# A hybrid block on one core: RG-LRU in its own buffers behind the RWKV's blocks, both pairs of heads in one PSUM bank, six banks for the late output-projection tiles

## The chip, the cores and the metric

The kernel runs on one core of a Trainium2 chip. The metric is the device time of one execution in microseconds (us). Of the kernel before, three runs are shown beside one profiled execution, whose trace gives every instruction of every engine: TensorE (PE, with its weight loads PEld), VectorE (DVE), ScalarE (ACT), GpSimd (POOL), and SyncE (SP), on whose queue nearly all DMAs are issued.

## What is computed

One layer over 2048 tokens, with 16 learned meta tokens put ahead of them, in float32 and of width 1024:

```python
p = rms_norm(h, norm_mix_pre) @ w_in                 # 1024 -> 3080 columns
oa = rg_lru_group(xa, ya, ...)                       # RG-LRU, 256 wide
ob = forgetting_attention_group(q, k, v, f, ...)     # 8 heads of 64, causal, with decay
oc = rwkv7_group(pc, ...)                            # 4 heads of 64, delta rule
h = h + rms_norm(concat(oa, ob, oc) @ w_out, norm_mix_post)
f = causal_dwconv(rms_norm(h, norm_ffn_pre) @ ffn_up, ffn_conv)      # 1024 -> 2 x 2816, 3 taps
h = h + rms_norm((gelu(gate) * val) @ ffn_down, norm_ffn_post)
```

The RG-LRU is a 4-tap convolution `u`, two gates (block-diagonal products with `u`), and a scan `h = a h + sqrt(1 - a^2) (i u)`, times `gelu(ya)`. The RWKV-7 group updates a 64 x 64 state per head and token with a decay, a removal along `kk` and an addition.

## The kernel before, in words

Every large product is made of three single-pass products of split operands (hi x hi, hi x lo, lo x hi; `mm3`, L148 to L152). The stages follow each other in one program, and the builder puts the instructions of each engine in an order of its own: by their place in the program and by when a model of the machine has their operands ready. On the chip every engine takes its list strictly in that order.

**Input projection** (to about 850 us). The tokens are done in three parts. In each part, `w_in_norm` (L165) normalises and transposes the rows, and `w_in_part` (L258) goes through the column blocks: RWKV's eight, RG-LRU's four, then k, v and q. Each unit loads 512 KB of weights, splits them, and multiplies. Results go to scratch in DRAM.

**Recurrences beside it.** `Beside` (L1856) runs a generator, `recurrences` (L1886), whose every `yield` ends one step; after each unit of the projection `advance` takes PACE = 1.5 steps on average. A part has 25 units; its own recurrences are added at unit 14, so that 12 units of each part, and the first 13 of the next, have its steps put beside them. For each part there are two steps of gates for the attention and then three blocks of 256 tokens. For each block:

- `lru_block` (L1333): two steps. The convolution `u`, the two gate products L1359 and L1363, tanh, exp, a square root (L1378), the scan (L1382), and the product with gelu (L1386 to L1391). The gate products and scans are made for each half of the channels (p = 0, 1); everything else runs on both halves at once, 512 elements wide. It borrows the RWKV's buffers `k`, `r`, `sq`, `e` and `raw`.
- `Rwkv.block` (L955): four steps up to SOLVED. `mixed` shifts tokens; L981 and L987 are the decay's and the rate's products, L995 and L1014 those of the norm of the keys, L1034 that of the bonus. Each of the pairs p = 0, 1 of heads takes the bank from `pe()` in turn: there is one, with tag `ae` (L935), so that a product waits until the reader of the one before is through. Then `chunks` (L1039): scores (L1058), transposes (L1087), and a 16-step substitution (L1099 to L1102).
- the ending of the block before: seven steps, from L1111 to the mixed output at L1282, with the state's steps at L1209.

With the two RG-LRU steps a block makes 13 steps. What remains when the projection ends is run by `beside.finish()`, in program order ahead of the attention.

While parts 2 and 3 run, `up_sums` (L1544) makes sums and differences of the up projection's weights for eleven column blocks on POOL: one step loads two tiles of 512 KB, makes four sums, and writes 1 MB; one step is taken in every fourth unit.

**Attention** (about 860 to 1590 us). `Attn.run` goes through the heads twice, first for the queries of blocks 0 and 1, then for 2 and 3 (512 queries each). The products of scores (L635, L636) fall into two banks with tag `sc`, the maxima's into `mx`, the values' into `pv`. The exponentials (L640) go into a ring `p` of NP = 9 buffers of 128 x 512, and are summed by POOL and DVE (L679). Between the two halves `meta` (L543) does the 16 meta rows in buffers of their own.

**Output projection** (`w_out_tile`, L1421), 17 tiles: 2 rows, then 16 of 128. Tiles 0 to 8 need only the first half of the attention and fill its second half; tiles 7 and 8 are held back for its last steps. A tile loads the mixed rows (`load_parts`, L139: ACT's copy L144 and DVE's difference L145 into `mh` and `ml`, two buffers each), makes two halves of 512 columns, and `add_normed` (L1444) squares both (L1450, into `mh` as waste), adds the sums (L1451), takes 1/sqrt by an integer guess and three Newton steps on DVE (`rstd_from`, L80 to L90: nine operations on 128 x 1), scales (L1456) and adds the residual (L1457). `rstd_of` (L93) does the same for the next norm (its square, L96, again into `mh`). `Banks` (L1399) hands out the banks: two, and from tile 8 on three. From tile 8 on, `ffn_norm` (L1484) also prepares the up projection's operands, one tile of rows at a time, and `ffn_sums` (L1517) subtracts the quarters on POOL.

**Up and down projection** (to the end). `ffn_up` (L1643) goes through 3 x 22 units of seven products with three banks each, in turn from two pools; the first unit takes the pool that lies where the output projection's banks were. `Down` (L1756) then makes 8 pairs of row tiles in two passes; `add_normed` closes each tile of the second.

## Time and profile before

| | us |
|---|---|
| runs of the kernel before, median of 3 | 3098.33 |
| lowest and highest | 3095.21 and 3101.57 |
| the profiled execution | 3089.22 |
| its span, first to last instruction | 3087.5 |
| mean granted PE clock | 0.962 |

In the page of the profile, busy time is given per engine with its share of the span and the number of instructions; the rows of digits cut the span into 40 slices of 77 us. The granted clock tells at what share of its full speed PE was let run. In the rows of waits stand the waiting engine, tile and line, what ended the wait, the total in us, how often, and the longest. In the timeline stand the start, the length, the engine, the line, the operation, the tiles (out<-in), and in brackets the engine's idle time just before, with what ended it. Tile names are the program's: `eps` is the bank of `pe()`, `rw...` are the RWKV's buffers, `pswo` the output projection's banks, `psu` the up projection's.

### The profile page before, as it was taken

The numbers are of one execution on the slowest core, as the hardware profiler recorded it, in microseconds if no ns is written. First come the engines' busy times: TensorE is split into PE (matmuls) and PEld (weight loads), VectorE is DVE, ScalarE is ACT, GpSimd is POOL, SyncE is SP. The second block draws the span as 40 slices with busy tenths as digits, with TensorE's granted clock in tenths as the row PEclk, the third lists the DMA queues.
The fourth block names the chain that finished last, engine by engine and source line by source line (L and its number), as shares of the span: only waits on it lengthen the run. The fifth ranks groups of instructions, "written<-read, shape, count | busy, mean of one in ns | idle before, by whom it ended". The sixth has DMA issues, their size and how long they took to land. (4 is left out here: it accounts for less than half of the span.)

```text
span 3087.5 us, 52530 instructions
## 1 busy us (share of the span) xinstructions
PE 2920.0 (95%) x18488; PEld 2490.5 (81%) x18488; DVE 2230.6 (72%) x4574; ACT 1458.1 (47%) x2716; POOL 1320.6 (43%) x1447
## 2 busy tenths in 40 slices
PE   6998999999978899999998899999999999999998
PEld 6997898988856554665576899999999999787776
DVE  5258666777678778778748788787778787547777
ACT  4245333444534444445533556656566665324332
POOL 1001211232124465556733457445645534557665
PEclk9998999999958888999999999999999999999999
DMA  4345544475353335544236456566777765425444
GB/s 142 115 134 166 154 122 133 145 207 170 84 125 76 81 84 136 140 111 115 64 106 201 154 183 181 173 195 209 212 213 215 214 193 180 159 99 169 148 157 143
DMA packets 482520, 463.92 MB, mean 150 GB/s; under 512 B 83808, under 2 KB 391722, under 8 KB 479296
## 3 DMA queue, kind: packets, MB, share of 16 engines
q1 hardware_dynamic: 481872, 460.18, 50.9%
q8 instruction: 145, 2.38, 0.3%
q14 instruction: 119, 0.97, 0.1%
q0 software_dynamic: 384, 0.39, 0.0%
HBM read 334.58 MB, written 125.87 MB: 149 GB/s over the span
## 5 line engine op out<-in xcount | busy, mean ns | idle before, releaser
L150 PE MATMUL psu<-xo,uw 128*128 128x344 f32 x1848 | 590.1, 324 | 14.9 <-DVE wx L1457 4.8
L151 PE MATMUL psu<-xo,uw 128*128 128x344 f32 x1848 | 594.1, 322 | 1.0 <-DVE xo L1529 1.0
L152 PE MATMUL psu<-xo,uw 128*128 128x344 f32 x1848 | 583.4, 321 | 0.0
L152 PE MATMUL psp<-xh,wl 128*128 128x384 f32 (+2 forms) x1152 | 377.3, 328 | 0.0
L150 PE MATMUL psp<-xh,wh 128*128 128x384 f32 (+2 forms) x1152 | 377.3, 328 | 0.0
L151 PE MATMUL psp<-xl,wh 128*128 128x384 f32 (+2 forms) x1152 | 376.9, 327 | 0.0
L150 PEld LDWEIGHTS psu<-xo,uw 128*128 128x128 f32 x1848 | 348.0, 189 | 18.1 <-DVE wx L1457 5.2
L1529 DVE TENSOR_TENSOR uw<-uq,uw 128x512 fp32r<-128x512 f32 x341 | 313.6, 926 | 62.4 <-ACT uw L1528 59.2
L151 PEld LDWEIGHTS psu<-xo,uw 128*128 128x128 f32 x1848 | 349.3, 189 | 1.3 <-DVE xo L1529 1.3
L152 PEld LDWEIGHTS psu<-xo,uw 128*128 128x128 f32 x1848 | 347.8, 189 | 0.0
L1528 ACT ACTIVATE uw<-uq 128x512 fp32r<-128x512 f32 x462 | 287.4, 627 | 107.3 <-PE psu L152 50.6
L640 ACT ACTIVATE p<-sc,bias 128x512 f32<-128x512 f32 (+4 forms) x352 | 197.9, 591 | 206.8 <-PE sc L636 160.8
L1660 DVE SCALAR_TENSOR_TENSOR uy<-psu,ffn_cols,uy 128x342 f32<-128x342 f32 (+1 forms) x396 | 223.6, 567 | 73.1 <-ACT uy L1658 71.9
L679 POOL TENSOR_TENSOR acc<-acc,p 128x512 f32<-128x512 f32 (+3 forms) x208 | 230.3, 1113 | 101.9 <-DVE acc L679 50.4
L1666 POOL TENSOR_TENSOR uy<-uy,uy 128x342 f32<-128x342 f32 (+1 forms) x132 | 141.9, 1075 | 270.5 <-DVE uy L1660 78.9
L1529 POOL TENSOR_TENSOR uw<-uq,uw 128x512 fp32r<-128x512 f32 x121 | 175.6, 1451 | 140.6 <-ACT uw L1528 115.9
L151 PEld LDWEIGHTS psp<-xl,wh 128*128 128x128 f32 x1152 | 217.9, 189 | 7.3 <-issue 5.4
L152 PEld LDWEIGHTS psp<-xh,wl 128*128 128x128 f32 x1152 | 218.0, 189 | 6.7 <-issue 4.9
L150 PEld LDWEIGHTS psp<-xh,wh 128*128 128x128 f32 x1152 | 217.9, 189 | 6.2 <-issue 4.0
L512 DVE TENSOR_REDUCE mc<-mx 128x1 f32<-128x400 f32 (+5 forms) x320 | 171.8, 554 | 58.9 <-PE mx L509 53.2
L1528 ACT ACTIVATE fo<-u 128x896 fp32r<-128x896 f32 x88 | 81.1, 922 | 231.1 <-POOL u L1776 123.5
L1529 DVE TENSOR_TENSOR fo<-u,fo 128x896 fp32r<-128x896 f32 x88 | 103.0, 1172 | 116.1 <-ACT fo L1528 116.1
(453 smaller groups left out, 6628.1 us busy)
## 6 DMA issues: line engine op xcount, KB each, us to landing
uq<-scr_us SPq DMA_DIRECT2D x220, 256.0 KB
uq<-in_ffn_up_dram SPq DMA_DIRECT2D x209, 256.0 KB
raw<-in_w_in_dram SPq DMA_DIRECT2D x72, 512.0 KB
u<-scr_ff SPq DMA_DIRECT2D x88, 256.0 KB
scr_ff<-uy SPq DMA_DIRECT2D x110, 171.0 KB
q<-scr_qh SPq DMA_DIRECT2D x96, 128.0 KB
us<-in_ffn_up_dram SPq DMA_DIRECT2D x22, 512.0 KB
scr_us<-us SPq DMA_DIRECT2D x11, 1024.0 KB
```

The lines of the kernel that those rows point to most:

```text
L150: nc.tensor.matmul(out, ah, bh, start=first, stop=False, skip_group_check=more)
L151: nc.tensor.matmul(out, ah, bl, start=False, stop=False, skip_group_check=more)
L152: nc.tensor.matmul(out, al, bh, start=False, stop=last, skip_group_check=more)
L512: self.reduced = nc.vector.tensor_reduce(mc[:rows, i, ci : ci + 1], ps[:rows, :full], axis=AX.X, op=ALU.max)
L640: last = nc.scalar.activation(p[:rows, :w], ps[:rows, :w], AF.Exp, bias=bias[:rows, j : j + 1])
L679: eng.tensor_tensor(a, ps_[0][0][:rows, c0:n] if start and i == 1 else a, p[:rows, : n - c0], op=ALU.add)
L1528: core.nc.scalar.activation(hi, src, AF.Copy)
L1529: (eng or core.nc.vector).tensor_tensor(lo, src, hi, op=ALU.subtract)
L1660: stt(y[:, :n], src[:, i : n + i], cw[:, 44 * i + cc : 44 * i + cc + 1], y[:, :n], op0=ALU.mult, op1=ALU.add)
L1666: core.pooled = nc.gpsimd.tensor_tensor(v[:, :n], g[:, :n], v[:, :n], op=ALU.mult)
```

## The change

1. `lru_block` now does one half of the channels after the other in four steps, in buffers of its own (`lu`, `lr`, `lg`, `la`, 256 wide, and `lraw`), with both gate products of a half in one bank; and in `recurrences` it stands behind the block and the ending, not ahead of them.
2. In `Rwkv.block` both products of a pair go to the two halves of one bank before either is read; the bonus is one product of 512 columns. With the RG-LRU's that makes 7 turns of the `ae` bank a block in place of 13.
3. PACE is 2.0 in place of 1.5; a block now makes 15 steps.
4. `up_sums` works on half a column block at a time, in half the buffer: 22 steps of four loads, four sums of 256 elements and one write, a step in every second unit.
5. `meta` takes its five larger tiles from the exponentials' ring `p`.
6. From tile 8 on, `Banks` goes round six banks: three of the up projection's first pool, then the two and the one of before. The up projection's first unit takes that first pool (`turn = 1`).
7. From tile 8 on and in the down projection (`core.root`), 1/sqrt is made by DVE (mean), ACT (square root) and DVE (reciprocal).

```diff
+def rstd_root(core, v, sums, width):
+    nc = core.nc
+    ms, y = v[:, 0:1], v[:, 2:3]
+    nc.vector.tensor_scalar(ms, sums[1], 1.0 / width, EPS, op0=ALU.mult, op1=ALU.add)
+    nc.scalar.activation(y, sums[0], AF.Sqrt, scale=1.0 / width, bias=ms)
+    nc.vector.reciprocal(y, y)
+    return y
...
     ss = v[:, 4:5]
+    if core.root:
+        half = width // 2
+        sums = ss, v[:, 5:6]
+        for i, acc in enumerate(sums):
+            cs = slice(half * i, half * i + half)
+            core.nc.scalar.activation(junk[:, cs], src[:, cs], AF.Square, accum_out=acc)
+        return rstd_root(core, v, sums, width)
...
-        new = lambda s: self.t([P, NH, META], s, F32R, 1)
-        q1, q2, q3, k1, k2 = (new("m" + s) for s in ("q1", "q2", "q3", "k1", "k2"))
-        v = self.t([META, NH, 64], "mv", bufs=1)
+        new = lambda shape, dt: self.t(shape, "p", dt, self.NP)
+        q, k = new([P, 3, NH, META], F32R), new([P, 2, NH, META], F32R)
+        (q1, q2, q3), (k1, k2) = (q[:, i] for i in range(3)), (k[:, i] for i in range(2))
+        v = new([META, NH, 64], F32)
...
+        both = lambda ps: [ps[:, p * n : p * n + n] for p in range(2)]
+        for rows, s, out in ((slice(0, 64), "w0_h", sig), (slice(64, 128), "a0_h", av)):
+            ps = both(self.pe())
+            for p in range(2):
+                nc.tensor.matmul(ps[p], k["up"][rows, P * p : P * p + P], flat(wa[:])[rows], start=True, stop=True)
+            for p in range(2):
+                nc.scalar.activation(flat(half(out, p)), ps[p], AF.Tanh, scale=0.5, bias=pcol(s, p))
...
-            ps = self.pe()
-            nc.tensor.matmul(ps[:, :n], k["bones"][:], flat(half(kp, p)), start=True, stop=True)
-            tt(half(bon, p), ps[:, :n].rearrange("p (c t) -> p c t", t=CH), half(rav, p)[:, :, 2], op=ALU.mult)
+        ps = self.pe()[:, : 2 * n]
+        nc.tensor.matmul(ps, k["bones"][:], flat(kp[:]), start=True, stop=True)
+        tt(bon[:], ps.rearrange("p (c t) -> p c t", t=CH), rav[:, :, 2], op=ALU.mult)
...
     def tl(s):
-        return R.t([P, 2, 256], s)[:, :, :n]
+        return R.t([P, 256], s)[:, :n]
...
+    def raw(row, a):
+        t = R.t([P, 260], "lraw", bufs=2)[:, : c0 + n - a]
+        nc.sync.dma_start(t, scr["p"][row : row + P, a : c0 + n])
+        return t
...
     for p in range(2):
         pc = slice(p, p + 1)
+        x = raw(P * p, c0 - 3)
+        u, r, g, al = (tl("l" + s) for s in ("u", "r", "g", "a"))
...
+        pa, px = ps[:, :n], ps[:, 256 : 256 + n]
+        nc.tensor.matmul(pa, k["ga_w"][:, p], u, start=True, stop=True)
+        nc.tensor.matmul(px, k["gx_w"][:, p], u, start=True, stop=True)
...
     def next(self):
-        self.turn = (self.turn + 1) % 3 if self.wide else 0
-        third = self.turn == 2
-        return self.pools[third].tile([P, 512], F32, tag="wo", name=self.core.n("pswo"), bufs=1 if third else 2)
+        if not self.wide:
+            pool, tag, n = self.pools[-2]
+        else:
+            self.turn += 1
+            ring = [p for p in self.pools for _ in range(p[2])]
+            pool, tag, n = ring[self.turn % len(ring)]
+        return pool.tile([P, 512], F32, tag=tag, name=self.core.n("pswo"), bufs=n)
...
+    n = HK // 2
+    for j, z in ((j, n * i) for j in js for i in range(2)):
+        t = pool.tile([P, 4, n, P], F32, tag="us", name=core.n("us"))
+        for i in range(4):
+            r0, c0 = P * (HK * (i % 2) + z), FF * (i // 2) + P * j
+            nc.sync.dma_start(t[:, i], w_up[r0 : r0 + n * P, c0 : c0 + P].rearrange("(k p) c -> p k c", p=P))
...
-    turn = 0
+    turn = 1
...
-PACE = 1.5
+PACE = 2.0
...
     for b in ((0, 1, 2), (3, 4, 5), (6, 7, 8))[part]:
-        yield from lru_block(core, R, scr, lk, b)
         gen = R.block(b)
         while next(gen) != R.SOLVED:
             yield
         yield from R.ending
         R.ending = gen
+        yield from lru_block(core, R, scr, lk, b)
...
-                    if part and i % 4 == 0:
+                    if part and i % 2 == 0:
...
-            banks = Banks(core, ps_wo)
+            banks = Banks(core, [(ps_f[0], "up", 3), (ps_wo[0], "wo", 2), (ps_wo[1], "wo", 1)])
...
-                banks.wide = i >= LATE - 1
+                banks.wide = core.root = i >= LATE - 1
```

More of the change, by code (lines that the diff above doesn't have):

```diff
@@ L45, in __init__ @@
         self.flip = 0
+        self.root = False
     def n(self, s):
@@ L1011, in block @@
         tt(kp[:], kt[:], kp[:], op=ALU.mult)
+        ps = both(self.pe())
         for p in range(2):
[L1013 to L1015 removed]
+            nc.tensor.matmul(ps[p], k["spr"][:, p], kinv, start=True, stop=True)
+        for p in range(2):
+            stt(flat(half(kt, p)), flat(half(kt, p)), pcol("k_k", p), ps[p], op0=ALU.mult, op1=ALU.mult)
         kk = kt[:]
```

110 lines of the change are left out of this document (40 added, 70 removed).

## The prediction

> **What bounds the kernel now.** I read the page first. TensorE (PE) is busy 95% of the span, and the digits show where it isn't: slices 12 to 16, a little in slices 4 and 22, and both ends.
>
> ```profile
> PE 2920.0 (95%) x18488; PEld 2490.5 (81%) x18488; DVE 2230.6 (72%) x4574; ACT 1458.1 (47%) x2716; POOL 1320.6 (43%) x1447
> PE   6998999999978899999998899999999999999998
> PEclk9998999999958888999999999999999999999999
> ```
>
> Busy time alone hides the clock, so I cut the span at the stages' borders and read the table of windows: length, then busy us and instructions of PE, weight loads, DVE, ACT and POOL, then PE's granted clock.
>
> ```profile
> 40.00:275.00 235.00, 234.88 (x1334) 226.66 (x1333) 105.20 (x216) 87.93 (x150) 7.59 (x17) 1.00 0.42 124
> 275.00:310.00 35.00, 22.77 (x105) 19.34 (x104) 30.12 (x66) 19.50 (x35) 7.28 (x6) 0.76 0.69 196
> 310.00:620.00 310.00, 304.66 (x2674) 276.40 (x2674) 200.25 (x433) 126.72 (x224) 60.43 (x75) 0.99 0.48 140
> 620.00:850.00 230.00, 227.31 (x2371) 205.89 (x2365) 164.89 (x360) 104.26 (x191) 49.97 (x60) 0.99 0.54 152
> 850.00:1190.00 340.00, 294.51 (x2365) 196.53 (x2363) 267.79 (x815) 141.36 (x300) 148.79 (x236) 0.78 0.40 96
> 1190.00:1590.00 400.00, 380.51 (x1648) 228.20 (x1649) 298.13 (x700) 199.75 (x353) 247.04 (x265) 0.99 0.42 105
> 1590.00:1725.00 135.00, 114.78 (x516) 94.10 (x514) 108.10 (x244) 51.95 (x94) 34.40 (x27) 0.92 0.53 173
> 1725.00:2610.00 885.00, 877.21 (x5550) 874.71 (x5549) 699.42 (x1093) 546.08 (x1077) 469.07 (x376) 1.00 0.65 196
> 2610.00:3087.00 477.00, 446.97 (x1879) 355.02 (x1877) 324.24 (x497) 163.02 (x262) 285.21 (x359) 0.97 0.45 149
> ```
>
> I call length minus busy times clock the loss: time in which PE did no work at full clock. Beside the input projection (310 to 850) it is 540 - 0.99 x 532 = 13 us, 0.025 a us. In 850 to 1190, where the RWKV's last blocks run beside the attention's first half, it is 340 - 0.78 x 294.5 = 110 us, 0.32 a us, with DVE at 79%. Beside attention and output projection (1190 to 1590) it is 23 us, 0.06 a us. The late tiles (1590 to 1725) lose 135 - 0.92 x 114.8 = 29 us, and the seam of the first two parts (275 to 310) 35 - 0.76 x 22.8 = 18 us. Since the change leaves PE's work almost as it is, only these losses can move. PE's waits, longest first, name some of them.
>
> ```profile
> PE eps L981 <- ACT rwe L982: 12.5, 2, 11.9
> PE pswo L150 <- DVE wx L1457: 11.1, 4, 4.4
> PE psu L150 <- DVE wx L1457: 4.8, 1, 4.8
> ```
>
> **The change, part by part.** *The seam.* The timeline at 287 us shows the longest wait whole.
>
> ```profile
> 285.90 0.68 DVE L1391 SCALAR_TENSOR_TENSOR rwk<-rwk,rwe 128x512 f32<-128x512 f32 x1
> 286.61 0.47 ACT L982 ACTIVATE rwe<-eps,rwkv_om 128x256 f32<-128x256 f32 x1 [2.34 <-DVE rwk L1391]
> 287.14 1.22 PE L981 MATMUL eps<-rwwa,wa_up 64*128 64x256 f32 x2 [11.87 <-ACT rwe L982]
> ```
>
> L1391 is the RG-LRU's last operation, and it reads buffer e. L982 writes the block's first part of e, so it waits for L1391; the second L981 waits for the one bank that L982 reads; all of PE stands behind it. With e no longer shared and one bank for both halves this wait goes, up to 16 of the 18 us. But the next part's norms stand behind it and are late next. I take half: -8 (0 to -16).
>
> *The tail.* These rows give the RWKV's pace: first product of the gates of blocks 6, 7 and 8 (L981), the RG-LRU ahead of block 6 (L1359), two halves of a pair at L981 and at L1034, and the last operation of the recurrence.
>
> ```profile
> 748.24 0.59 PE L1034 MATMUL eps<-rwsq,bones 128*128 128x256 f32 x2
> 767.92 0.59 PE L1034 MATMUL eps<-rwsq,bones 128*128 128x256 f32 x2
> 795.92 0.70 PE L1359 MATMUL eps<-rwk,lru_ga_w 128*128 128x256 f32 x2
> 812.62 0.70 PE L981 MATMUL eps<-rwwa,wa_up 64*128 64x256 f32 x2
> 822.62 0.70 PE L981 MATMUL eps<-rwwa,wa_up 64*128 64x256 f32 x2
> 898.38 1.22 PE L981 MATMUL eps<-rwwa,wa_up 64*128 64x256 f32 x2
> 986.72 0.69 PE L981 MATMUL eps<-rwwa,wa_up 64*128 64x64 f32 x2
> 1180.35 0.20 DVE L1278 TENSOR_TENSOR rwxu<-rwxu,rps 128x64 f32<-128x64 f32 x1
> ```
>
> A block takes 86 and 88 us. The RG-LRU ahead of it is 17 of them (796 to 813), since both use buffers k, r, sq and e; the halves of a pair stand 10 us (L981) and 20 us (L1034) apart, for the bank has to be read in between. A block's 13 turns of that bank become 7. By the written order, 18 steps are put beside the projection's last 12 units, about 4 of them owed to the part before, and they reach block 6 and six of the seven steps of block 5's ending. Afterwards there are 24 with none owed, which reach block 7's solve and three steps of block 6's ending: some 10 of RWKV's 11 steps further, about 80 us of chain. Moved from beside attention to beside the projection, each us brings 0.32 less what its work loses elsewhere (0.68 x 0.05), 0.286: -23. The bounds are 0, if DVE's load and not RWKV's place sets the tail, and -48 for twice the distance.
>
> *The RG-LRU itself.* Ten wide DVE operations and five wide ACT ones a block become twice as many half ones, and each half has its own square root, so each of nine blocks has two table loads more there and back.
>
> ```profile
> L1391 DVE SCALAR_TENSOR_TENSOR rwk<-rwk,rwe x9: 216/680/930, 196.7 to 994.2; 128x512 f32<-128x512 f32 x7, 128x416 f32<-128x416 f32 x1, 128x128 f32<-128x128 f32 x1
> L1361 DVE TENSOR_SCALAR rwe<-eps,lru_cols x18: 268/476/484, 175.0 to 982.5; 128x256 f32<-128x256 f32 x14, 128x208 f32<-128x208 f32 x2, 128x64 f32<-128x64 f32 x2
> L1378 ACT ACT_TABLE_LOAD x9 | 11.5, 1283 | 18.5 <-DVE rwr L1377 18.4
> ```
>
> On DVE 20 x 0.476 - 10 x 0.68 = 2.7 us a block, on ACT two loads, 2.6 us. Beside the projection both lie in idle time of DVE (365 busy of 540) and ACT; in the tail one full block and a small one stay: +3 (0 to +10). The Trainium skill, in "ScalarE: Activation LUTs" under "Table sets: the hidden batching unit", speaks against this: functions are to be grouped by table set, and a switch is put at 2.66 us with its drain. The trace agrees on the load, 1283 ns, and no row here shows a drain; four more switches in the tail at the page's figure would be 11 us, an estimate, and the sum 8 us smaller.
>
> *The late tiles.* With three banks a tile's second half waits for the last tile's first half (11.1 us), and the up projection's first unit for the last tile (4.8 us). Six banks, and that unit on the three freed first, take both away. DVE's chain shortens too: from L1451 to the last L89 it took 1.9 us undisturbed and 6.7 us while POOL worked on the quarters' sums.
>
> ```profile
> 1658.79 0.16 DVE L1451 TENSOR_TENSOR rs<-rs 128x1 f32<-128x1 f32 x1 [0.33 <-ACT mh L1450]
> 1665.34 0.83 DVE L89 SCALAR_TENSOR_TENSOR rs<-rs 128x1 f32<-128x1 f32 x1
> 1700.71 0.16 DVE L1451 TENSOR_TENSOR rs<-rs 128x1 f32<-128x1 f32 x1 [3.28 <-ACT mh L1450]
> 1702.49 0.16 DVE L89 SCALAR_TENSOR_TENSOR rs<-rs 128x1 f32<-128x1 f32 x1
> L150 PE MATMUL pswo<-woh,mh 128*128 128x512 f32 x122 | 50.4, 413 | 11.1 <-DVE wx L1457 11.1
> ```
>
> Ten operations become two with a square root between. What adds a wait: ACT's root now stands behind DVE, and ACT's copies of mh behind the root. Late next is mh: two buffers, the older read last by L96. I take 13 of the 15.9 us and half of the 9 us of half clock: -17 (-8 to -27). Tile 8 now needs banks that the attention's scores hold, so it fills no gap there; 48 products of 0.41 us bound that at +20 (they overlap, so it is less), 0 if attention ends sooner for it, as I assume: it then has PE to itself.
>
> *The meta rows.* Their operands now take five of the nine buffers of the exponentials.
>
> ```profile
> L562 PE MATMUL mx<-mk,mq x8: 170/170/253, 1144.3 to 1144.5; 128*16 128x16 f32 x8
> L587 PE MATMUL mx<-mp,mv x16: 204/204/225, 1159.1 to 1160.8; 16*64 16x16 f32 x16
> ```
>
> They hold them for these 17 us and the loads before, while attention makes do with four: between 0 and all 17. I take +6.
>
> *Costed at nothing.* The up sums in halves:
>
> ```profile
> L1559 POOL TENSOR_TENSOR us<-us 128x512 f32<-128x512 f32 x33 | 49.1, 1487 | 2.2
> SPq L1560 <- POOL us L1559: 18.1, 6, 5.7
> L1552 SPq DMA_DIRECT2D us<-in_ffn_up_dram x22: 378/582/2078, 287.2 to 752.4; - x22
> ```
>
> POOL is idle 430 of 540 us, so 44 more, shorter operations hide there. SP gets 77 issues more here and 27 for the RG-LRU, 104 x 0.58 = 60 us in 700; behind a write that waits for POOL (up to 5.7 us) stand the projection's weights, which are loaded ahead. Without that cover a few us. The root in the last stage is worth -1 in the final chain (+2 to -2).
>
> **Sum**, against the profiled execution (3089.2 us, span 3087.5): -8 - 23 + 3 - 17 + 6 - 1 = -40. That execution lies 9.1 us below the median of the runs, so 3098.3 - 40 = 3058.
>
> **Rivals.** *The tail doesn't shrink* (0.20): attention's first half is held by its own DVE reductions, not by the RWKV beside it. For it speaks DVE's 79%; against it that the RWKV's operations are part of this load. Seam, late tiles and costs remain, with the seam halved again: -4 + 3 - 17 + 6 - 1 = -13, 3085 (3078 to 3102).
>
> *PE stops behind the recurrence* (0.19, slower): steps come at 2.0 a unit in place of 1.5, and PE takes its stream in order; a recurrence product placed ahead of its operands stops the projection, as at 287 us: 11.87 us idle and 0.24 x 22.8 = 5.5 us of clock, 17 in all. Against it: that stop came from the shared e, and 310 to 850 lost only 13 us in all. From the third such stop on it eats the 40 us; with four it gives 3058 + 68 = 3126.
>
> *The six banks bring nothing* (0.07): tiles stay bound to the two buffers of mh and the wait moves from the bank to L145. Then -17 becomes about 0: 3075. And 0.03 is for no change from all that cancels.
>
> **How the numbers follow.** My forecast has 0.51 (3028 to 3083). A measurement of this kernel can tell about 0.2%, 6 us, from no change. Faster: 0.51 + 0.16 of the first rival + 0.07 = 0.74; within 0.2%: 0.04 + 0.03 = 0.07; slower 0.19. The range, 3025 to 3108, leaves out the far end of the tail's gain (0.07) and the worse half of the stops (0.12).
>
> **What would show it.** The wait of L981 for L982 gone, and the clock in 275 to 310 up; block 8's L981 before about 910 instead of 987, and the recurrence's end before 1110; the loss in the stretch from the projection's end to 1190 nearer 85 than 110; no PE wait for wx in the late tiles, tile 16's products ending about 15 us sooner counted from attention's last exponential. I am wrong if the recurrence's end moves and the tail's loss doesn't, or if idle time grows in 310 to 850.

## The result, and the profile after

The changed kernel took 3108.79 us (median of 8 runs, 3105.01 to 3116.63), the kernel before on the same chip 3095.22 us (8 runs, 3091.01 to 3101.57): a ratio of 1.0044 (95% interval 1.0029 to 1.0059). It is slower by 14 us where 40 us less was forecast, and lies 0.8 us above the range. The profiled execution took 3106.46 us, with a span of 3104.7 and a mean granted clock of 0.957.

The page's rows that answer to those of before: TensorE's busy time, then its digits and those of the clock.

```profile
PE 2924.9 (94%) x18470; PEld 2500.8 (81%) x18470; DVE 2188.1 (70%) x4401; ACT 1497.1 (48%) x2833; POOL 1324.0 (43%) x1491
...
PE   6998999999989978999889899999999999999998
...
PEclk9999999989978788999999999999999999999999
```

TensorE is as busy as before, within 5 us; slice 9 (621 to 698 us), beside the projection, had a 9 in the clock and now has an 8. The windows, cut at the changed kernel's own borders (the projection ends at 867, attention's last scores come at 1604, the up projection ends at 2633):

```profile
275.00:310.00 35.00, 26.23 (x312) 22.67 (x311) 28.78 (x73) 19.75 (x37) 13.28 (x19) 0.80 0.73 202
310.00:620.00 310.00, 304.76 (x2534) 276.13 (x2532) 193.61 (x449) 129.19 (x232) 56.67 (x86) 0.99 0.45 133
620.00:867.00 247.00, 237.72 (x2346) 217.98 (x2343) 170.77 (x395) 120.60 (x225) 52.88 (x79) 0.96 0.55 154
867.00:1207.00 340.00, 289.29 (x2338) 194.90 (x2337) 274.18 (x834) 153.80 (x321) 144.19 (x234) 0.79 0.43 104
1207.00:1604.00 397.00, 367.82 (x1544) 217.03 (x1544) 276.46 (x654) 189.27 (x337) 240.44 (x263) 0.96 0.38 91
```

The loss (length minus busy time at full clock, as in the prediction) is 35 - 0.80 x 26.23 = 14 us at the seam (18 before), 8 in 310 to 620 (8), but 247 - 0.96 x 237.72 = 19 from 620 to the projection's end (5), 340 - 0.79 x 289.29 = 111 in the next 340 us (110), and 397 - 0.96 x 367.82 = 44 in the attention's second half (23). So the loss of those 340 us stood still, and two stretches that the forecast had left alone lost 14 and 21 us more. Cut where the recurrence itself ends, the tail reads otherwise: the kernel before up to 1180 and from there to the last scores, then the changed kernel up to 1152 and in the next 55 us.

```profile
850.00:1180.00 330.00, 286.16 (x2329) 192.42 (x2327) 259.75 (x799) 136.34 (x292) 141.93 (x230) 0.78 0.39 93
1180.00:1587.00 407.00, 385.86 (x1668) 230.94 (x1668) 303.97 (x712) 203.79 (x359) 253.71 (x270) 0.99 0.43 108
```
```profile
867.00:1152.00 285.00, 249.88 (x2155) 173.56 (x2153) 236.24 (x742) 133.18 (x285) 129.37 (x211) 0.78 0.39 93
1152.00:1207.00 55.00, 39.40 (x183) 21.34 (x184) 37.95 (x93) 20.62 (x36) 14.82 (x23) 0.79 0.62 163
```

Beside the recurrence the loss is 330 - 0.78 x 286.16 = 107 us before and 285 - 0.78 x 249.88 = 90 us after, 0.32 a us in both. Behind it the kernel before loses 407 - 0.99 x 385.86 = 25 us, but the changed kernel 55 - 0.79 x 39.40 = 24 us in the first 55 us alone, and the 44 in the rest. So the price per us held as long as the recurrence ran; what did not hold is that the attention runs almost without loss where the recurrence is gone.

Stage by stage, each from the last product of one kind to the last of the next in the profiled execution (us):

| | projection ends | recurrence ends | attention | late tiles | up | down | tail | span |
|---|---|---|---|---|---|---|---|---|
| before | 850.0 | 1180.6 | 737.1 | 112.5 | 911.1 | 463.3 | 13.5 | 3087.5 |
| after | 867.4 | 1152.4 | 736.3 | 123.5 | 905.9 | 460.6 | 11.0 | 3104.7 |
| e1 (tile 8 on old banks) | 874.7 | 1159.1 | 736.7 | 110.2 | 909.9 | 457.6 | 11.0 | 3100.1 |
| e14 (six banks, root only) | 852.7 | 1182.5 | 725.1 | 110.2 | 906.1 | 458.6 | 11.1 | 3063.8 |
| e15 (e1, no sums) | 841.9 | 1148.2 | 747.4 | 111.1 | 928.6 | 463.1 | 11.2 | 3103.3 |
| e18 (e1, sums whole) | 863.7 | 1139.9 | 729.1 | 110.3 | 908.8 | 459.6 | 11.4 | 3082.9 |

Of TensorE's longest waits after, over the whole span; then its longest from 310 us to the projection's end; then three rows of the timeline: the stop at the seam, the start of block 8's gates, and the recurrence's last operation.

```profile
PE pst L139 <- DVE xt L126: 18.9, 5, 11.5
...
PE pswo L168 <- ACT mh L162: 6.6, 2, 3.7
PE rps L1107 <- DVE rs L85: 6.4, 1, 6.4
```

```profile
PE rps L1145 <- DVE rwxu L1175: 2.6, 1, 2.6
PE psp L170 <- DVE wl L163: 2.6, 1, 2.6
PE rps L1145 <- POOL us L1581: 2.5, 1, 2.5
PE rps L1145 <- DVE rwxu L1161: 2.4, 3, 1.9
```

```profile
289.04 1.08 PE L1107 MATMUL rps<-ident,rwbk 128*128 128x128 f32 x4 [6.36 <-DVE rs L85]
982.73 0.66 PE L1003 MATMUL eps<-rwwa,wa_up 64*128 64x64 f32 x4
1152.13 0.22 DVE L1298 TENSOR_TENSOR rwxu<-rwxu,rps 128x64 f32<-128x64 f32 x1
```

The wait of the gates for the RG-LRU's reader (11.87 us before) is gone, and so is the late tiles' wait for wx (11.1). In their places stand a wait of 6.36 us at the seam, where DVE works on the next part's norms (L85), one of 6.6 us for mh in the late tiles, and beside the projection short stops, most of them at the recurrence's products L1145. Block 8's gates start at 983 (987 before) and the recurrence ends at 1152 (1181), where I had called for 910 and for less than 1110.

### The profile page after: what moved, and what is told of

The parts are those of the page before. It is cut to its first block, busy times and chain, and to the rows that moved or that the text cites. A ratio compares the mean times of both kernels' runs of the same rounds, so it can differ in the third digit from the quotient of the medians.

```text
span 3104.7 us, 52679 instructions
## 1 busy us (share of the span) xinstructions
PE 2924.9 (94%) x18470; PEld 2500.8 (81%) x18470; DVE 2188.1 (70%) x4401; ACT 1497.1 (48%) x2833; POOL 1324.0 (43%) x1491
## 4 chain that ended last, share of the span: by engine, by line
PE 39%; DVE 5%; DMA 4%; POOL 3%; issue 2%; ACT 1%; SPq 0%; POOLq 0%; DVEq 0%; ACTq 0%
PE psu L168 8%; PE psu L169 8%; PE psu L170 8%; PE psd L170 2%; PE psd L168 2%; PE psd L169 2%; DMA u<-scr_ff 2%; PE po L678 1%; PE pswo L168 1%; PE pswo L169 1%; PE pswo L170 1%; DVE fo L1553 1%; DMA xt<-scr_h 1%; DVE uw L1553 1%; PE sc L655 1%
## 5 line engine op out<-in xcount | busy, mean ns | idle before, releaser
L1553 DVE TENSOR_TENSOR fo<-u,fo 128x896 fp32r<-128x896 f32 x88 | 109.5, 1244 | 119.6 <-ACT fo L1552 119.5
```

What stands on the lines that cost most here:

```text
L1553: (eng or core.nc.vector).tensor_tensor(lo, src, hi, op=ALU.subtract)
```

## The experiments

All ratios are to the kernel before on the same chip, with 95% intervals. A difference of two ratios is taken in us by the 3096 us or so of the kernel before; it is uncertain by some 0.2 to 0.3%, 6 to 9 us. The ends of the stages are read from one profiled execution each. The changed kernel, e1, e7 and e8 have the same projection and the same sums, and their projections end at 867 to 875; differences below 8 us there mean little.

### Late tiles: e1, e3, e8, e14

**e1**: the changed kernel, with tile 8 on the two old banks and the six from tile 9 on.

```diff
-        self.core, self.pools, self.wide, self.turn = core, pools, False, -1
+        self.core, self.pools, self.wide, self.turn = core, pools, False, 1
...
-                banks.wide = core.root = i >= LATE - 1
+                core.root, banks.wide = i >= LATE - 1, i >= LATE
```

> The changed kernel, but tile 8 of the output projection keeps the two old banks and the six begin with tile 9. Theory (tile 8 lost its place): in the changed kernel tile 8 waits for the banks of the attention's scores, so some 14 us of PE work move behind the attention, and the attention does not end sooner for it. With tile 8 back it fills the attention's last steps: last score to last tile product falls from 123 to about 110 us, and the time by 8 to 14 us against the changed kernel, to 0.9995 to 1.002 of the kernel before. Rival (the attention is late for reasons of its own, as the buffers of the meta rows): the work moves back but the attention ends later by as much, time unchanged at 1.0044.

Measured: 3099.29 us, 0.9995 (0.9981 to 1.0009): tile 8's banks account for some 15 us (1.0044 - 0.9995), as much as the whole slowdown. Where, the windows of the output projection's products alone tell (attention of after, then of e1), and those of everything in the late stage (after, then e1).

```profile
867.00:1604.00 737.00, 98.22 (x384) 66.53 (x384) 19.38 (x29) 10.88 (x32) 0.88 0.40 97
```
```profile
875.00:1611.00 736.00, 98.03 (x384) 66.64 (x384) 18.81 (x28) 10.88 (x32) 0.89 0.40 97
```
```profile
1604.00:1727.00 123.00, 112.96 (x512) 91.07 (x509) 66.83 (x116) 47.94 (x112) 28.38 (x26) 0.94 0.60 185
```
```profile
1611.00:1722.00 111.00, 110.59 (x519) 88.98 (x519) 66.31 (x117) 48.73 (x115) 29.84 (x28) 1.00 0.63 205
```

In both kernels 384 products, eight tiles, run beside the attention: on the old banks tile 8 does not come back in there, against the theory (the kernel before has 450 products there). The gain lies behind the attention, where 123 - 0.94 x 112.96 = 17 us of loss became none. What stopped TensorE in the changed kernel is in its timeline, first TensorE, then ScalarE:

```profile
1613.40 0.79 PE L168 MATMUL pswo<-woh,mh 128*128 128x512 f32 x1 [2.91 <-ACT mh L162]
1643.76 0.80 PE L168 MATMUL pswo<-woh,mh 128*128 128x512 f32 x1 [3.67 <-ACT mh L162]
```
```profile
1636.06 1.28 ACT L99 ACT_TABLE_LOAD   x1
1637.36 0.30 ACT L99 ACTIVATE rs<-rs 128x1 f32<-128x1 f32 x1
...
1641.89 0.63 ACT L112 ACTIVATE mh<-wx 128x512 fp32r<-128x512 f32 x1 [1.17 <-DVE wx L1481]
1642.43 0.19 ACT L112 ACTIVATION_READ_ACCUMULATOR mh<-wx 128x1 f32 x1
1642.65 1.06 ACT L162 ACTIVATE mh<-raw 128x1024 fp32r<-128x1024 f32 x1
```

At the second stop the copy into mh for the next tile stands on ScalarE behind the root and the squares of the tile before, and these wait for DVE's wx: the added wait that the prediction named ("ACT's copies of mh behind the root"). The first stop is another: tile 8's copy starts at 1612.29, when its load lands, and that load is issued at 1607.64 only, 4 us behind the last scores, so that the tile begins 9.7 us behind them (3.3 us in e1). Why the load goes out so late there isn't shown. In e1 no stop is left.

**e3**: the kernel before with the six banks alone, and tile 8 on them (the diff's `Banks` and `turn = 1`).

> The kernel before with the six banks from tile 8 on and the up projection's first unit on the first pool; nothing else, the Newton steps stay. Theory (tile 8 lost its place): waits for wx go (16 us), tile 8's 14 us come behind the attention: last score to last tile product about 115 to 122 us (112 before), but the first unit of the up projection starts before that end; in all 0 to +6 us. Rival (the prediction's own step): 13 us less wait and 4 us of clock, ratio 0.995.

Measured: 3105.34 us, 1.0012 (0.9996 to 1.0028). The attention took 723.8 us, 13 less than before, with 384 products of the output projection beside it in place of 450; the late stage took 136.1, 24 more and more than the theory's 122, with 27 us of loss in it (17 before). Six banks from tile 8 on take no loss away without the root.

**e8**: e1 with the Newton steps instead of the root.

```diff
-                core.root, banks.wide = i >= LATE - 1, i >= LATE
+                banks.wide = i >= LATE
```

> As e1, with 1/sqrt again by the integer guess and three Newton steps on DVE, in the late tiles and in the down projection. Theory (the root shortens the chain that ends a late tile, as predicted): late stage 115 to 121 in place of 110, tail after the last product 13.5 in place of 11, ratio 1.001 to 1.004. Rival (with six banks nothing waits for that chain): late stage 109 to 112, ratio 0.999 to 1.001.

Measured: 3113.98 us, 1.0057 (1.0037 to 1.0077): the root is worth some 19 us of the changed kernel's time (1.0057 - 0.9995), 11 of them in the late stage (121.6 against 110.2), 4 in the down projection and 2.5 in the tail. The theory held, with a larger sum than I gave it; the stages left over differ by +5 (attention) and -3.5 us (up).

**e14**: the kernel before with e1's banks and the root, and nothing else of the change.

> The kernel before with the six banks from tile 9 on (tile 8 on the two old ones) and the square root on ACT from tile 8 on and in the down projection; nothing else of the change. Theory (what the change brings lies behind the attention alone): projection and attention as before, late stage 107 to 112 in place of 112.5, down projection 456 to 460 in place of 463, tail 11, ratio 0.995 to 0.998. Rival (the two bring nothing by themselves): ratio 0.999 to 1.002.

Measured: 3064.54 us (3052.83 to 3078.52), **0.9901 (0.9878 to 0.9924)**: faster than both kernels, beyond what I expected. One window of its late stage:

```profile
1578.00:1688.00 110.00, 109.83 (x512) 88.30 (x513) 65.64 (x116) 47.98 (x113) 29.43 (x27) 1.00 0.64 207
```

Not a stop is left, with tile 8 among the late tiles. Against before the profiled stages differ by +3 (projection), -12 (attention, with 66 products fewer beside it), -2 (late, with these 66 in it), -5 (up), -5 (down) and -2.5 (tail). The up projection's first unit no longer waits for wx (4.8 us before), but 11 us behind the last tile's last product TensorE stops for 6.9 us for the operand xo, in e14 as in the changed kernel. The first 40 us of the stage lose 40 - 0.87 x 31.95 = 12 us before and 40 - 0.91 x 30.92 = 12 in e14, so this wait was moved and not removed.

### The pace and the pairs: e2, e4, e5, e6

**e2**: the changed kernel with `PACE = 1.5`; **e5**: the kernel before with `PACE = 2.0`.

> The changed kernel with 1.5 steps a unit instead of 2.0. Theory (PE stops behind the recurrence because steps come too early): the projection, which ends at 867 us instead of 850, ends at 853 to 858, loss between 620 and its end falls from 19 to about 8 us; the recurrence ends later than 1149; time down by 5 to 12 us if what is left for the tail costs nothing more. Rival (the stops come from the order, RG-LRU behind the block, or from POOL's halved sums): the projection still ends at 865 or later, and the time is the same or higher, since more of the recurrence is left beside the attention.

> The kernel before with 2.0 steps a unit in place of 1.5, nothing else. Theory (the pace only trades: steps put sooner cost the projection what they save the attention, as with 1.5 in the changed kernel, where the projection ended 10 us sooner and the attention took 10 us more): projection's end 855 to 862 in place of 850, attention's stage 727 to 732 in place of 737, ratio 0.999 to 1.001. Rival (the pace itself makes the stops and gains nothing): projection's end 860 or later, attention's stage unchanged, ratio 1.003 or more.

Measured: e2 3116.37 us, 1.0048 (1.0030 to 1.0066); e5 3095.45 us, 0.9993 (0.9975 to 1.0012). In e2 the projection ended 10 us sooner and the attention took 10 more; in e5 it ended 5 us later and the attention took 3 less. The pace only trades; it is not what stops TensorE: e2 keeps 21 us of loss between 620 and the projection's end, where the theory had about 8.

**e4**: the kernel before with both products of a pair of heads in one bank (the diff's part 2).

> The kernel before with both products of a pair of heads in one bank, nothing else (RG-LRU ahead of the block, in shared buffers, pace 1.5). Theory (the cycle of the blocks is set by the ending and the two score buffers): first gate product to bonus product shrinks from 45 to 71 us to 30 to 40, but the blocks still follow each other in 84 to 95 us in the tail, the recurrence ends within 15 us of 1180, time within 6 us. Rival (turns of the bank are on the cycle): cycle 60 to 70 us, recurrence ends before 1140, time 10 us or more lower.

Measured: 3124.28 us, 1.0075 (1.0054 to 1.0096). A block came from its gates to its bonus in 32 to 53 us instead of 52 to 84, but blocks hardly followed faster (gates of 6, 7, 8 at 831, 901, 1000; before at 813, 898, 987), and the projection ended at 871. So the theory held for the cycle (70 and 99 us, 85 on average) and missed the time: the recurrence ended at 1203, not within 15 us of 1180, and 23 us were lost.

**e6**: e1 with the pairs in turns again.

> The changed kernel with tile 8 on the two old banks (as e1), and the RWKV's two pairs of heads again in turns of the bank, one after the other. Theory (both products of a pair at once make PE stop in the projection, as in e4): the projection ends at 855 to 862 in place of 875, attention's stage 735 to 742, ratio 0.993 to 0.997. Rival (the RG-LRU in halves behind the ending makes the stops): the projection ends at 868 or later, ratio 0.999 or more.

Measured: 3136.77 us, 1.0128 (1.0103 to 1.0153), the projection's end 885.2. The theory is out, and the rival's bounds are passed by far: pairs in one bank cost the kernel before some 23 us, but save the changed one some 40 (1.0128 - 0.9995). What a part costs depends on the others.

### Meta rows and RG-LRU: e7, e9, e10, e12

**e10**: the kernel before with the meta rows in the ring (the diff's part 5).

> The kernel before with the meta rows' operands in the ring of the exponentials, nothing else. Theory (the ring costs the attention some 13 us around the meta rows): TensorE's idle time in the stretch from 280 to 360 us after the projection's end 17 us or more in place of 7, attention's stage 745 to 752 in place of 737, ratio 1.003 to 1.005. Rival (that idle time comes with the recurrence's last endings): idle time 7 to 10, attention's stage 734 to 740, ratio 0.999 to 1.001.

Measured: 3098.50 us, 1.0011 (0.9997 to 1.0024); attention 740.7 us. The theory of 13 us is out; the 3 to 4 us can't be told from none, nor from the predicted 6.

**e7**: e1 with the meta rows in buffers of their own.

> As e1, and the meta rows again in buffers of their own, so that the exponentials keep their nine. Theory (the ring holds the attention up around the meta rows): TensorE's idle time in the stretch from 280 to 360 us after the projection's end falls from 23 us to 8 to 12, attention's stage 724 to 730 in place of 737, ratio 0.995 to 0.997. Rival (that idle time belongs to the last endings of the recurrence and only stands at the same place): idle time there 18 or more, ratio 0.999 to 1.001.

Measured: 3182.43 us, 1.0281 (1.0251 to 1.0310), and for a reason of its own: with these buffers the attention's space reaches into the recurrence's. Its SP queue, the recurrence's last write and the attention's first load:

```profile
1077.66 0.38 SPq L1299 DMA_DIRECT2D scr_mix<-rwxu  x1
1078.09 0.47 SPq L488 DMA_DIRECT2D k<-scr_kh  x1
```

In e1 that first load goes out at 880.67. So e7 says nothing on the ring's cost. That the two spaces overlap is read from this order; it would say why the ring was used: it makes room for the RG-LRU's buffers.

**e9**: the kernel before without the RG-LRU.

```diff
-    raw = R.raw(0, c0 - 3, c0 + n)
...
+    yield
+    nc.sync.dma_start(scr["mix"][0:256, t0 : t0 + n], scr["p"][0:256, c0 : c0 + n])
     yield
```

> The kernel before with the RG-LRU left out: its two steps stay, but one DMA hands its input xa on as its output, so that the first 256 columns of the mixed rows are not the reference's. Theory (a block's cycle is set by its ending and the two buffers of scores, and the RG-LRU runs beside it): the gates of blocks 6, 7 and 8 still start 78 to 88 us apart, and the recurrence ends at 1150 to 1180. Rival, the step of the prediction (17 of a block's 86 to 88 us are the RG-LRU's): they start 66 to 74 us apart and the recurrence ends before 1110. The time falls in either case with the work that is left out, ratio 0.985 to 0.995.

Measured: 3111.06 us, 1.0056 (1.0037 to 1.0075), slower with less to do, where both sides had called for 0.985 to 0.995. Gates of blocks 6, 7 and 8 at 799.8, 865.0 and 949.3: 65 and 84 us apart, between theory and rival; so the RG-LRU is in the cycle, with some 12 of its 17 us on average. The recurrence ended at 1150, 31 us sooner. Did the attention gain by it? The first 340 us after the projection's end, in e9 and then in e15:

```profile
857.00:1197.00 340.00, 297.06 (x2427) 196.31 (x2426) 264.06 (x777) 135.51 (x284) 155.59 (x247) 0.81 0.45 106
```
```profile
842.00:1182.00 340.00, 286.10 (x2296) 194.76 (x2295) 259.64 (x794) 148.57 (x308) 145.09 (x229) 0.76 0.40 97
```

Losses of 340 - 0.81 x 297.06 = 99 and 340 - 0.76 x 286.10 = 123 us, where the recurrence ended 292 and 306 us after the projection; before it was 110 at 331, after 111 at 285. By 0.32 a us they should lose 97 (e9), 102 (e15) and 95 (after). e9 fits, the two others are 21 and 16 us off, and e9's attention is no shorter either (740.0), for its second half lost what the first gained.

**e12**: the kernel before with the RG-LRU in halves behind the ending; the sums in halves and the ring come with it for room (the diff's parts 1, 4 and 5).

> The kernel before with the RG-LRU in halves, in buffers of its own, in four steps behind the block and the ending; with it come what makes room for its buffers, the sums in halves and the meta rows in the ring. Pairs in turns, pace 1.5, three banks and Newton steps stay. Theory (its gate products stand in PE's list ahead of their convolution, as in e6, where they waited 10.7 us): the projection's end 865 to 885, recurrence's end 1170 to 1200, ratio 1.007 to 1.013. Rival (in e6 it was the pace together with the turns of the bank): the projection's end 857 or sooner, ratio 1.005 or less, all of it the ring's.

Measured: 3160.70 us, 1.0204 (1.0180 to 1.0227), the projection's end 869.4, the attention 783.9: The projection ends where the theory had it, but the attention's stage is 47 us longer, which neither side expected. The gate products' wait is not among the longest. e11, whose edit is part of this one, loses 1.74 of these 2.04% by itself.

### The sums: e11, e13, e15, e16, e17, e18

**e11**: the kernel before with the up projection's sums in halves (the diff's part 4), nothing else.

> The kernel before with the sums for the up projection in halves of a column block, one step in every second unit, nothing else. Theory (hidden on POOL, as predicted): the projection's end 849 to 853, ratio 0.999 to 1.001. Rival (POOL takes its list in order, and the recurrence's operations that stand behind a sum make PE stop): waits of the recurrence's products for POOL 5 us or more, the projection's end 856 or later, ratio 1.002 or more.

Measured: 3151.73 us, 1.0174 (1.0146 to 1.0202), **55 us slower** for the edit that I had costed at nothing. By the profiled stages about half of it lies in the projection, which ends at 879 in place of 850, and the other half in the attention, 768.8 us in place of 737.1, where no sum is made. The rival's ratio and its projection's end hold; of its 5 us of waits for POOL there are 2.7. POOL's timeline, then TensorE's, then the windows ahead of and behind that moment (PEclk is the first of the last three numbers):

```profile
470.07 0.55 POOL L1101 TENSOR_TENSOR rwitmp<-rwix,rwia 128x72 f32<-128x72 f32 x1 [0.49 <-DVE rwix L1102]
473.97 0.72 POOL L1555 TENSOR_TENSOR us<-us 128x256 f32<-128x256 f32 x1 [3.35 <-DMA us<-in_ffn_up_dram]
474.65 0.40 POOL L1101 TENSOR_TENSOR rwitmp<-rwix,rwia 128x80 f32<-128x80 f32 x1
475.01 0.72 POOL L1557 TENSOR_TENSOR us<-us 128x256 f32<-128x256 f32 x1
475.69 0.41 POOL L1101 TENSOR_TENSOR rwitmp<-rwix,rwia 128x88 f32<-128x88 f32 x1
```
```profile
476.12 3.33 PE L1125 MATMUL rps<-rwxu 32*32 32x32 f32 x96 [2.71 <-POOL rwitmp L1101]
```
```profile
466.00:476.00 10.00, 7.41 (x99) 6.52 (x98) 6.09 (x19) 3.39 (x6) 4.49 (x10) 1.00 0.69 194
476.00:487.00 11.00, 10.88 (x146) 10.29 (x147) 6.18 (x14) 0.00 (x0) 4.76 (x8) 0.53 0.47 137
```

A sum (L1555) stands in POOL's list between two steps of the substitution (L1101) and waits 3.35 us for its load; the substitution is late, a recurrence's product in TensorE's list waits 2.71 us for POOL, and the next 11 us run at a clock of 0.53. The stop costs 2.7 + 0.47 x 10.88 = 7.8 us. From 310 us to the projection's end there are eight stops of 1.2 to 3.7 us, and the loss is 310 - 0.96 x 302.58 = 20 and, from 620 to 879, 259 - 0.96 x 247.50 = 21 us, where the kernel before has 8 and 5. Of the eight only this stop is put down to POOL, the others to DVE and ACT; and POOL waits long for these loads in the kernel before too (nine waits of together 148 us from 310 on, sixteen of 173 in e11). So that the sums in halves make the loss is shown by the edit, the path by one stop. The changed kernel has the same picture once: its POOL and TensorE.

```profile
669.23 0.32 POOL L1121 TENSOR_TENSOR rwitmp<-rwix,rwia 128x48 f32<-128x48 f32 x1 [0.31 <-DVE rwix L1122]
670.81 0.74 POOL L1579 TENSOR_TENSOR us<-us 128x256 f32<-128x256 f32 x1 [1.26 <-DMA us<-in_ffn_up_dram]
671.50 0.34 POOL L1121 TENSOR_TENSOR rwitmp<-rwix,rwia 128x56 f32<-128x56 f32 x1
671.80 0.74 POOL L1581 TENSOR_TENSOR us<-us 128x256 f32<-128x256 f32 x1
```
```profile
675.04 3.35 PE L1145 MATMUL rps<-rwxu 32*32 32x32 f32 x96 [2.55 <-POOL us L1581]
```

Here DVE idles for 1.76 us until POOL's step at 671.50 is through, then works without a pause, and its last operation on rwxu ahead of this product (L1155) comes at 674.16.

**e13**: e11 with two of the smaller buffers, so that loads can run ahead (`pool(p1a, "us", 2)`).

> As e11, but with two of the half-sized buffers, so that a step's loads need not wait for the write of the step before (as much memory as the kernel before uses). Theory (in e11 a sum stands in POOL's list ahead of the recurrence's substitution, waits there for its load, and holds up what stands behind it): POOL's waits for these loads fall from 106 us to 60 or less, the projection ends at 860 or sooner in place of 879, ratio 0.999 to 1.008. Rival (it is the number of operations and DMA issues): the projection's end stays at 870 or later, ratio 1.013 or more.

Measured: 3138.99 us, 1.0142 (1.0123 to 1.0162), the projection's end 868.4. It took 13 of the 55 us back, so the one buffer is a part only. The theory is out on all three counts: POOL's waits for these loads did not fall. The rival's ratio holds, and its projection's end is missed by 2 us.

**e15** and **e16**: e1 and the kernel before, both without sums beside the projection (`EARLY = range(0)`).

> As e1, with no sums made beside the projection; the up projection makes all of them itself, so its stage is longer by some us in this kernel and in e16 alike. Theory (the sums in halves are the change's largest loss): the projection ends at 858 or sooner in place of 875, and this kernel is faster than e16 or equal, ratio to it 1.000 or less. Rival (the RG-LRU's place and the pairs make the stops, with or without the sums): the projection ends at 868 or later, ratio to e16 1.004 or more.

> The kernel before with no sums made beside the projection, as the measure for e15. Theory (the sums in whole blocks cost the projection nothing): projection's end 845 to 851 in place of 850, attention 735 to 740, the up projection's stage longer than 911. Rival (they cost something already in the kernel before): projection's end 843 or sooner.

Measured: e15 3107.54 us, 1.0039 (1.0025 to 1.0053); e16 3111.54 us, 1.0052 (1.0036 to 1.0069). The up projection, which then makes all sums itself, takes 19 to 21 us more in both. The windows of e15 ahead of the projection's end:

```profile
310.00:620.00 310.00, 308.20 (x2592) 279.25 (x2590) 194.66 (x469) 135.09 (x241) 22.05 (x44) 1.00 0.37 107
620.00:842.00 222.00, 221.87 (x2282) 203.87 (x2282) 155.01 (x372) 114.91 (x213) 21.13 (x40) 0.99 0.41 113
```

The theory of e15 held (0.9987 to e16). Without the sums the changed kernel's projection runs at full speed: 2 + 2 us of loss, its end at 842 where e1's is at 875. In the kernel before the sums cost the projection nothing (849 against 850). So whole sums fit the old order of the recurrence, and the sums in halves cost the new one's projection 33 us. In the whole, leaving them out brings nothing (1.0039 against e1's 0.9995): the up projection takes 19 us more, the attention 11.

**e17** and **e18**: e1 with the sums in whole blocks again. To make room, the forget gate's raw weights lie in the space of the results (e17) or in the ring of the weights' loads (e18).

```diff
-    raw = pools["w"].tile([P, KD, 8], F32, tag="fraw", name=core.n("fraw"), bufs=1)
+    raw = pools["nt"].tile([P, KD, 8], F32, tag="nt_x", name=core.n("fraw"))
```

> As e1, with the sums again made in whole column blocks, one step in every fourth unit, as in the kernel before; a small buffer of the forget gate's weights is laid into another's space to make room. Theory (the sums in halves alone keep the projection of the changed kernel from gaining): the projection ends at 838 to 852 in place of 875, attention 735 to 747, ratio 0.986 to 0.992. Rival (whole sums stop this order of the recurrence as well): the projection ends at 860 or later, ratio 0.995 or more.

> As e17, but the forget gate's weights lie in the ring of the weights' loads, not in the space of the results. Theory (in e17 TensorE's stop of 8 and 3 us with 17 us of half clock at 618 to 631 came from that buffer, and whole sums do not stop the projection): the projection ends at 845 to 860 in place of 876, ratio 0.986 to 0.993. Rival (whole sums or the new order make that stop, wherever the buffer lies): the projection ends at 868 or later, ratio 0.995 or more.

Measured: e17 3083.80 us, 0.9962 (0.9944 to 0.9981), the projection's end 875.9; e18 3086.21 us, 0.9959 (0.9941 to 0.9977), its end 863.7. e17's stop of 8 us at 626 came from the buffer that was moved, and is gone in e18, where only that buffer differs. There five stops of 1.6 to 2.9 us remain from 619 on, so that whole sums too cost the new order's projection 22 us (863.7 against 841.9), the halves 11 more (4 by the changed kernel's own 867). Both theories are out: that the halves alone keep the projection from gaining (e17), and that whole sums do not stop it (e18). Sums in whole blocks bring the changed kernel 11 us in all (0.9959 against e1's 0.9995).

## Why the prediction was wrong, point by point

Three pairs of runs and the result itself cut the change into four steps that add up:

| step (parts of the change) | runs | forecast, us | measured, us |
|---|---|---|---|
| six banks from tile 9 on, the root (6, 7) | e14 against before | -17 - 1 | -31 |
| RG-LRU, pairs, pace, meta rows (1, 2, 3, 5) | e18 against e14 | -8 - 23 + 3 + 6 = -22 | +18 |
| sums in halves (4) | e1 against e18 | 0 | +11 |
| tile 8 on the six banks (6) | after against e1 | 0 | +15 |
| together | after against before | -40 | +14 |

In another order the steps have other sizes: the sums alone cost 55 us, the pairs alone 23. And e18 also has the forget gate's weights elsewhere.

- **The tail, -23.** This is the step that failed worst: the recurrence's new place was to gain, and with the parts that make it, it cost 18 us: e18's projection ends 11 us later than e14's, its attention takes 4 us more and its up projection 3. It failed both ways. The recurrence ended 28 us sooner, where I had called for 70 or more: blocks 6, 7 and 8 follow each other in 84 and 91 us (86 and 88 before), though gates to bonus take 30 to 36 us instead of 64 to 75 and the RG-LRU is out of the way. And what it gained brought nothing: 111 us of loss against 110 in the 340 us. The 0.32 a us held beside the recurrence (107 us to 90), but the attention without it lost 68 us where it had lost 25. So the first rival was right that the tail doesn't shrink; that DVE's reductions hold it, its reason, wasn't tried. That a block's cycle is set by the ending of the block two before, through the two buffers of its scores, is argued from starts that follow each other (L1290 at 944.65, then the scores L1078 at 945.54). It wasn't tried with a third buffer, for which there is no room. (The bound of -48 is 46 by the prediction's own figures.)
- **The up sums, "costed at nothing" because "POOL is idle 430 of 540 us".** 11 us in the changed kernel (e1, e18), 55 us alone (e11). The cover was a share of busy time; what counts is POOL's order. I weighed SP's waits for POOL and overlooked POOL's own for its loads, with the recurrence's operations behind them.
- **The late tiles, -17.** The mechanism was right, and banks and root together bring more: in e14 the late and up stages together are 7 us shorter although 66 products, some 17 us of the 110 (432 products there, 366 before), have come into them. The root alone is worth 19 us in the changed kernel (e8). The 4.8 us of the up projection's first unit were not gained; 6.9 us for xo came in their place. In the changed kernel the two stages are 6 us longer. The step that failed is "0 if attention ends sooner for it, as I assume". In e3 and e14 the attention is 13 and 12 us shorter; in the changed kernel, with as few products of the output projection beside it, its second half lost 44 us instead of 23, and it isn't. Tile 8's place on the six banks cost 15 us more (e1): a stop for the mh that I had named as late next and priced too low, and one for tile 8's late load. (In the rows of the prediction DVE's slow chain lasts from 1658.79 to 1666.17, 7.4 us and not 6.7; the sum doesn't use it.)
- **The seam, -8.** -4 was measured (18 to 14): the next part's norms are late next, as said.
- **The meta rows, +6.** 3 to 4 (e10), with none and 6 within the error: not contradicted.
- **The root's last chain, -1.** -2.5 in the tail, and 3 to 6 less in the down projection. The first was the term's, the second I had not counted.
- **The RG-LRU itself, +3.** Not measured by itself; e15 shows that its operations fit beside the projection without a stop of 1 us or more. A table load takes 1.28 us here and nothing more: the one at 1636.06 starts 0.02 us behind the operation before it, and the activation 0.02 us behind the load. The drain that the Trainium skill adds ("ScalarE: Activation LUTs", "What ACT_TABLE_LOAD costs") doesn't show in these rows.
- **The rival of stops.** It happened (620 to 867: 19 us of loss, 5 before), by another cause than I gave: not the pace (e5, 0.9993), but the sums on POOL beside the new order of the recurrence (without sums 2 us from 620 on, e15; whole sums 22, e18).

What stays open: why the attention loses 68 us behind the recurrence's end in the changed kernel, 25 in the kernel before. Its second half loses 20 us more in e9 and e11 too, which share neither ring nor banks nor RG-LRU buffers with the changed kernel. Most of the 68 us lie at the border of the attention's two halves: 24 in the first 55 us and 63 - 0.86 x 55.80 = 15 in the next 63. From 1150 to 1160 TensorE is busy 1.3 of 10 us there, with waits of 3.4 us for DVE and of 4.4 us for a load of the meta rows. In the kernel before, whose meta rows (1144 to 1161) still have the recurrence's products beside them, it is busy all the time from 1150 to 1160. That the recurrence had filled this gap fits e9 and e15 too, whose recurrences also end early, but not e11 and e12, whose recurrences end late; it wasn't tried. The builder also makes another order of every engine for each of these kernels. Between e17 and e18, where only a small buffer differs, the attention's 709.6 and 729.1 us differ as much as most edits here bring; the runs don't tell which part of the order it is.

## What to carry to other kernels

Idle time of an engine hides an added operation only if nothing that another engine waits for stands behind it in its list: look for what is queued behind the operation's own wait, not for the share of busy time. A stop of TensorE cost its length and the slow clock after it (7.8 us for 2.7, e11). Before a time per us is taken from a stretch, check with rows in which its supposed cause differs that the two move together, and what the stretch loses once the cause is gone; and take a change of many parts apart, since here two of its seven parts, one of them mended in a line, make the fastest version.

## What the runs showed of the hardware

Stops of TensorE shorter than the slow clock that follows them: 2.71 us idle, then 11 us at a clock of 0.53 (e11). The Trainium skill ("TensorE: Matmul & The Clock Gate", "Part 1: The HAM clock gate") has the clock halved after at least one idle window of about 3.4 us; in this row a shorter stop was enough. By the clock's records half clock follows within 2 us on five of e11's eight stops (1.8 to 3.7 us long, for 3.4 to 10.2 us), and on the three others (1.2, 1.4 and 2.0 us) it doesn't. And taking work away can make a kernel slower: e9 leaves the whole RG-LRU out and takes 0.56% longer.
